# Sums of squares for the norms: four column chunks through selectors into one PSUM bank

## The chip, the cores and the metric

The kernel runs on one core of a Trainium2 chip, as one program with one launch. The metric is the device time of that execution in microseconds. Before the change three runs gave 1867.34, 1867.83 and 1867.99 us; the median is 1867.83 us.

The engines of the core are named as in the profile: PE (TensorE, matrix multiplies, with PEld for its weight loads), DVE (VectorE), ACT (ScalarE), POOL (GpSimd) and SP (SyncE, which here issues all DMA transfers, in order).

## The reference

Two layers over a residual stream of 1040 tokens (16 learned meta tokens and 1024 inputs) of width 1024.

- Layer 0: an RMS norm, one input projection, two kinds of attention side by side, a SiLU gate, an output projection and the residual add. The first attention is latent attention with 8 heads: queries and keys are made from low-rank latents which have norms of their own. The second is windowed attention over 128 tokens to each side, with 8 query heads and 2 key heads. Queries and keys of both have a norm per head.
- Layer 1: an RMS norm, an input projection, a short convolution, two gated linear recurrences (forward and backward), a SiLU gate, an output projection and the residual add.

All these norms need, for every token, the sum of the squares of a vector:

```
def rms_norm(x, g):
    xf = x.astype(jnp.float32)
    y = xf * lax.rsqrt(jnp.mean(xf * xf, axis=-1, keepdims=True) + EPS)
    return (y * g.astype(jnp.float32)).astype(x.dtype)
```

The inputs and the output are float32, and the sums must be precise.

## The kernel before, in words

**Layout.** Activations lie transposed: features on the 128 partitions, the 1040 tokens along the free dimension. A sum over features is thus a sum over partitions, and TensorE does it with a weight matrix of ones.

**Two-part numbers.** Matmuls run in a rounded float32 format. To keep precision, each operand is split into a high part and the rest (`hi`, `lo`), and a product is three matmuls; a sum of squares, whose weights are exact, needs two, one over `hi` and one over `lo`.

**Column pieces.** A PSUM bank holds 512 float32 per partition, so 1040 columns are cut in three: `C3` has 348, 346 and 346 columns, and `CH` has 272, 512 and 256 (`OFF` aligns these to banks in a three-bank tile).

**The stages**, in time: projections and up-projections of the latent attention (until about 200 us); projections, gates and the windowed attention in one mixed stream (until about 600 us); the dense latent attention with the output projection (until about 1218 us); the second layer.

**The sums of squares.** `stat(sq, s, m, dst, tag)` starts on L178. It splits the squares at once: POOL writes `sqh` (L182), VectorE writes `sql` (L183). It returns `later`, which the caller puts off: `put_off(n, fn)` and `tick()` count output tiles of the projections, so that the matmuls of the sum come one to four tiles behind. `later` then does, for each of three column pieces (L194 to L198): take a bank, two matmuls over `hi` and `lo`, one ScalarE copy of the piece into the row tile `sr`. At the end SP stores `sr` to a DRAM row (L199). `m` is 1, with a column of ones as weights (`one`), or 2, with `sel`, whose two columns select the partitions 0 to 63 and 64 to 127; there the squares of two heads have been folded into the halves by `fold`. Rows are read back in other shapes, for instance as 16 partitions of 65 tokens by `row_rsqrt` (L321) or with tokens on partitions by `tok_load` (L148) and `meta_col` (L297), get a reciprocal square root by Newton steps on VectorE (`newton_rsqrt`, L133 to L142), and go on as per-token scales.

There are 18 sums with a `tag`. Twelve belong to the first stage: input norm, two latents, shared rotary key, four query pairs and four key pairs. They use the two banks tagged `one`. Six belong to the windowed attention, namely two key norms (`d_sk`) and four query norms (`d_sq`). They use the tag `s`, whose two banks also hold the score tiles `sps` (L691 to L693). One more sum, for the second layer's norm (`d_vh`), has no tag: it uses a three-bank tile, six matmuls (`hi` first, then `lo`) and a single copy (L188 to L192).

**The order of the work.** In the first 1223 us the order on each engine is found by the framework's planner, from program order as priority and from costs of its own. Weight loads (`w_raw`, L94 to L97) and their splitting on POOL or VectorE (L115, L116) have a priority raised by 200 places. Within an engine instructions then run in that order. From the second tile of layer 1 on (L1367) the order of PE, DVE, ACT and POOL is written out by hand.

**A unit of the windowed attention** is two heads and 128 queries: scores on TensorE into `s` banks (L693), mask and maximum on VectorE (L694, L697), exponentials on ScalarE (L700, L703), reciprocal sums on VectorE (L706, L707), scaling on POOL (L710) and VectorE (L713), transposes on TensorE (L728, L731), their copies on ScalarE and VectorE (L736 to L742), and the product with the values (L753, L754). Between units TensorE does projections (`pj`, L168), whose outputs ScalarE (`qraw`, L327) or VectorE (`gt`, L783) takes out of the banks. `rope` is on L402 to L409.

Of the kernel before, what the change touches and what calls it, by code (L numbers as in the profile page):

```python
# [7 lines left out]
F32 = mybir.dt.float32  # L8
F32R = mybir.dt.float32r
# [7 lines left out]
P = 128  # L17
T = 1040
# [3 lines left out]
OFF = 240  # L22
C3 = ((0, 348), (348, 694), (694, 1040))
CH = ((0, 272), (272, 784), (784, 1040))
# [17 lines left out]
def trunk_kernel(ctx: ExitStack, tc: tile.TileContext, a: dict, out: bass.AP):  # L42
    nc = tc.nc
    wpool = ctx.enter_context(tc.tile_pool(name="wpool", bufs=3))
    xapool = ctx.enter_context(tc.tile_pool(name="xapool", bufs=16))
    const = ctx.enter_context(tc.tile_pool(name="const", bufs=1))
# [15 lines left out]
    def phase(psum_tags, **tags):  # L62

        es = ExitStack()
        stack.append(0)
        sb["P"] = es.enter_context(tc.tile_pool(name=f"ph{len(stack)}", bufs=1))
        sb["cnt"] = dict(tags)
        if psum_tags:
            psum(psum_tags)
        return es  # L70

    def row(nm, tag, dt=F32, w=T):
        if tag == "X":
            return xapool.tile([P, T], dt, tag="X", name=nm)
        return sb["P"].tile([P, w], dt, tag=tag, name=nm, bufs=sb["cnt"][tag])
# [8 lines left out]
    gqk = const.tile([P, 1], F32, name="gqk")  # L84
    nc.vector.tensor_mul(gqk, vcol(V_QKN_Q), vcol(V_QKN_K))

    ones1 = const.tile([P, 2], F32R, name="ones1")
    nc.vector.memset(ones1.bitcast(F32), 1.0)
    sel = const.tile([P, 2], F32R, name="sel")
    nc.vector.memset(sel.bitcast(F32), 0.0)  # L90
    nc.vector.memset(sel[0:64, 0:1].bitcast(F32), 1.0)
    nc.vector.memset(sel[64:128, 1:2].bitcast(F32), 1.0)

    def w_raw(src, n):  # L94
        raw = wpool.tile([P, 512], F32, tag="wr", name="wr", bufs=3)
# [59 lines left out]
    def big(nm="big"):  # L155
        return sb["ps"].tile([P, 1536], F32, tag="big", name=nm, bufs=sb["pcnt"]["big"])
# [18 lines left out]
    def bank(nm, tag):  # L175
        return sb["ps"].tile([P, 512], F32, tag=tag, name=nm, bufs=sb["pcnt"][tag])

    def stat(sq, s, m, dst, tag=None, rt="S"):  # L178

        hi = row("sqh", rt, F32R)  # L180
        lo = row("sql", rt, F32R)
        nc.gpsimd.tensor_scalar(hi, sq, 1.0, 1.0, ALU.mult, ALU.mult)  # L182
        nc.vector.tensor_sub(lo, sq, hi.bitcast(F32))  # L183

        def later():
            sr = row("sr", "T")
            if tag is None:
                ps = big("st")  # L188
                for j, x in enumerate((hi, lo)):
                    for c0, c1 in CH:  # L190
                        nc.tensor.matmul(ps[:m, OFF + c0:OFF + c1], s, x[:, c0:c1], start=j == 0, stop=j == 1)
                nc.scalar.copy(sr[:m], ps[:m, OFF:OFF + T])  # L192
            else:
                for c0, c1 in C3:  # L194
                    ps = bank("st", tag)
                    for j, x in enumerate((hi, lo)):
                        nc.tensor.matmul(ps[:m, :c1 - c0], s, x[:, c0:c1], start=j == 0, stop=j == 1)
                    nc.scalar.copy(sr[:m, c0:c1], ps[:m, :c1 - c0])  # L198
            nc.sync.dma_start(dst, sr[:m])  # L199

        return later

# [46 lines left out]

    rstd = const.tile([P, T], F32, name="rstd")  # L250
    ph = phase({"b": 2, "one": 2}, c=10, T=8, S=6, tab=2)
    one = ones1[:, 0:1]
    xh, xl, xraw = [], [], []
    w0 = {}
    sb["ahead"] = 0
# [9 lines left out]
    for k in range(8):  # L265
        h = row("xh", "X", F32R)
        lo = row("xl", "X", F32R)
# [5 lines left out]
    def proj1(e):  # L273
        ps = parts("pj")
        for hf in range(2):
            wh, wl = split_w(a["w1"][e, hf], (4, P), "w1")
            mm3p(ps, [(wh[:, k], wl[:, k], xh[4 * hf + k], xl[4 * hf + k]) for k in range(4)], hf == 0, hf == 1)
            if hf == 1:
                tick()
            yield 5.3 if hf == 0 else ps  # L280

    def run(g):
        r = None
        for v in g:
            if not isinstance(v, float):
                r = v
        return r
# [47 lines left out]
    for e in range(2):  # L335
        ps = first[3 + e]
# [49 lines left out]
    for e in range(3):  # L386
        ps = run(proj1(e))
        h = row("cqh", "c", F32R)
        lo = row("cql", "c", F32R)
# [21 lines left out]
    ps = run(proj1(5))  # L411
# [63 lines left out]
    for hf in range(2):  # L475
        wu = [split_w(a["uv"][hf, k], (512,), "wv") for k in range(2)]
        for i in range(9):
            c0, m = (0, NM) if i == 8 else (NM + P * i, P)
            ps = sb["ps"].tile([P, 512], F32, tag=f"b{i % 3}", name="vps", bufs=2)
# [426 lines left out]
    def parts_c(nm, third="t"):  # L906

        px = psC.tile([P, 1024], F32, tag="px", name="px" + nm, bufs=2)
        return [(px[:, 0:512], *C3[0]), (px[:, 512:1024], *C3[1]), (bank(nm, third), *C3[2])]
# [50 lines left out]
    for d in range(8):  # L960
        ps = parts_c("op")
# [162 lines left out]
    for d in range(1, 8):  # L1124
        ps = parts_c("op")
# [6 lines left out]
    def two(nm):  # L1132
        return sb["ps"].tile([P, 1024], F32, tag="two", name=nm, bufs=1)
# [33 lines left out]
    def halves(t, o=0):  # L1167
        return [(t[:, 0:512], o, o + 512), (t[:, 512:1024], o + 512, o + 1024)]
# [185 lines left out]
    def pair_of(nm):  # L1354
        ts = [bank(nm, "c") for _ in range(2)]
        return [(ts[j], 512 * j, 512 * j + 512) for j in range(2)]
# [170 lines left out]
    for d in range(3, 8):  # L1527
        if d % 3 == 1:
            ps = halves(two("oo"))
        elif d % 3 == 0:  # L1530
            ps = pair_of("oo")
        else:
            ps = halves(big("oo"))
# [101 lines left out]
```

## Time and profile before

| | |
|---|---|
| median of three runs | 1867.83 us |
| the profiled execution, whole | 1866.78 us |
| its span, first to last instruction | 1864.9 us |
| granted TensorE clock, mean | 0.997 |
| busy: PE / DVE / ACT / POOL | 97% / 66% / 47% / 43% |
| DMA, mean over the span | 100 GB/s |

Line numbers (L197) are those of the kernel file. A row of a waits view gives who waited, for whom, the total in us, how many times and the longest. A row of a timeline gives the start in us from the span's start, the time in us, engine, line, operation, output<-inputs, shapes, and in brackets how long the engine was idle before it and what ended that. Matmuls are pipelined: the time that one takes of TensorE is the distance between starts. A wait of PEld is a wait of the weight load, which is often hidden under the matmul before it. "PEld" and "PE" waits for the same thing are not to be added.

### The profile page before, as it was taken

How to read it: one execution, taken by the hardware profiler on the slowest of the kernel's cores; microseconds unless marked ns; L12 is line 12 of the kernel's file. 1: busy time of each engine (PE TensorE's matmuls, PEld its weight loads, DVE VectorE, ACT ScalarE, POOL GpSimd, SP SyncE). 2: the span in 40 equal slices, each digit the busy share in tenths (PEclk: the TensorE clock that was granted, in tenths of full speed). 3: DMA queues.
4: the chain of work that ended last, by engine and by line, in shares of the span. 5: the costliest groups of instructions: out<-in, count | busy, mean ns of one | idle time of the engine just before them, and what ended most of it. 6: DMA issues, size and time to landing. Idle time of an engine off the chain costs nothing.

```text
span 1864.9 us, 28561 instructions
## 1 busy us (share of the span) xinstructions
PE 1803.3 (97%) x10822; PEld 1641.8 (88%) x10822; DVE 1229.8 (66%) x1956; ACT 877.3 (47%) x1490; POOL 802.1 (43%) x713
## 2 busy tenths in 40 slices
PE   8999989989999999999999999999999999999999
PEld 7997888889999999888888889998888889988887
DVE  8687357787764641678777774348988989989000
ACT  5455224445443210466667652127776676674000
POOL 5446365354322463357555433332433433326331
PEclk9999999999999999999999999999999999999999
DMA  5355532223222363323222103422222222136421
GB/s 181 81 191 185 164 92 69 62 60 103 61 84 93 137 184 115 117 69 93 70 75 75 41 24 117 145 70 60 76 80 74 95 72 77 60 131 254 143 77 41
DMA packets 109333, 186.47 MB, mean 100 GB/s; under 512 B 31951, under 2 KB 51535, under 8 KB 109198
## 3 DMA queue, kind: packets, MB, share of 16 engines
q1 hardware_dynamic: 109198, 184.67, 31.2%
q8 instruction: 85, 1.39, 0.3%
q14 instruction: 50, 0.41, 0.1%
HBM read 126.72 MB, written 49.92 MB: 95 GB/s over the span
## 4 chain that ended last, share of the span: by engine, by line
PE 69%; DVE 16%; ACT 7%; POOL 5%; issue 2%; DMA 1%; SPq 0%; DVEq 0%; POOLq 0%; ACTq 0%
PE pj L168 12%; PE oo L168 10%; PE pxop L168 6%; PE pg L1183 5%; PE px L935 5%; PE pu L1183 5%; PE av L1026 4%; PE tp L998 3%; PE op L168 3%; PE up L168 3%; PE pz L128 2%; PE vps L435 2%; PE py L935 2%; DVE oxl L769 1%; DVE oz L1287 1%
## 5 line engine op out<-in xcount | busy, mean ns | idle before, releaser
L116 POOL TENSOR_TENSOR wl<-wr,wh 128x512 fp32r<-128x512 f32 (+2 forms) x218 | 320.8, 1475 | 301.9 <-ACT wh L113 269.8
L115 POOL TENSOR_SCALAR wh<-wr 128x512 fp32r<-128x512 f32 (+2 forms) x157 | 121.6, 775 | 376.0 <-PE pj L168 124.4
L168 PE MATMUL pj<-xh,wl 128*128 128x346 f32 (+1 forms) x768 | 251.3, 328 | 14.3 <-DVE wl L116 7.8
L168 PE MATMUL pj<-xl,wh 128*128 128x346 f32 (+1 forms) x768 | 249.1, 324 | 0.9 <-DVE xl L269 0.8
L168 PE MATMUL pj<-xh,wh 128*128 128x346 f32 (+1 forms) x768 | 248.9, 324 | 0.0
L168 PEld LDWEIGHTS pj<-xh,wl 128*128 128x128 f32 x768 | 146.5, 191 | 16.1 <-ACT xh L268 7.7
L168 PEld LDWEIGHTS pj<-xl,wh 128*128 128x128 f32 x768 | 146.6, 191 | 2.0 <-DVE xl L269 1.9
L168 PEld LDWEIGHTS pj<-xh,wh 128*128 128x128 f32 x768 | 146.6, 191 | 0.1
L1183 PE MATMUL pu<-h1h,wl 128*128 128x346 f32 (+1 forms) x384 | 125.2, 326 | 6.3 <-DVE ou L1201 3.3
L1183 PE MATMUL pu<-h1l,wh 128*128 128x346 f32 (+1 forms) x384 | 123.5, 322 | 0.0
L1183 PE MATMUL pu<-h1h,wh 128*128 128x346 f32 (+1 forms) x384 | 123.4, 321 | 0.0
L1013 ACT CAST pth<-tp 128x512 fp32r<-128x512 f32 (+1 forms) x160 | 77.9, 507 | 66.2 <-PE tp L998 52.3
L1014 DVE TENSOR_TENSOR ptl<-tp,pth 128x512 fp32r<-128x512 f32 (+1 forms) x160 | 90.2, 585 | 19.9 <-ACT pth L1013 16.4
L1183 PE MATMUL pg<-h1h,wl 128*128 128x512 f32 x256 | 101.4, 396 | 0.0
L168 PE MATMUL oo<-oyh,wh 128*128 128x512 f32 x256 | 101.1, 395 | 0.0
L1183 PE MATMUL pg<-h1h,wh 128*128 128x512 f32 x256 | 101.1, 395 | 0.0
L1183 PE MATMUL pg<-h1l,wh 128*128 128x512 f32 x256 | 100.8, 394 | 0.0
L168 PE MATMUL oo<-oyh,wl 128*128 128x512 f32 x256 | 100.6, 393 | 0.0
L168 PE MATMUL oo<-oyl,wh 128*128 128x512 f32 x256 | 100.4, 392 | 0.0
L944 ACT ACTIVATE p<-py,mmx,msc 128x256 f32<-128x256 f32 (+1 forms) x72 | 40.8, 567 | 119.0 <-DVE mmx L942 102.3
L1351 DVE TENSOR_TENSOR hres<-oo,hres 128x512 f32<-128x512 f32 x16 | 10.6, 688 | 129.0 <-PE oo L168 129.0
L998 PE MATMUL tp<-ident,p 128*128 128x128 f32 (+1 forms) x576 | 90.5, 275 | 2.7 <-POOL p L955 1.9
(446 smaller groups left out, 5471.2 us busy)
## 6 DMA issues: line engine op xcount, KB each, us to landing
wr<-in_w SPq DMA_DIRECT2D x128, 256.0 KB
wr<-in_wo SPq DMA_DIRECT2D x64, 256.0 KB
s_g<-gth SPq DMA_DIRECT2D x10, 520.0 KB
xr<-in_x SPq DMA_DIRECT2D x8, 520.0 KB
s_qn<-qr SPq DMA_DIRECT2D x8, 520.0 KB
s_kn<-kr SPq DMA_DIRECT2D x8, 520.0 KB
sw<-qraw SPq DMA_DIRECT2D x16, 260.0 KB
yb<-s_yb SPq DMA_DIRECT2D x8, 520.0 KB
```

The costliest lines, as they stand in the source:

```text
L115: eng.tensor_scalar(hi[:, :n], raw[:, :n], 1.0, 1.0, ALU.mult, ALU.mult)
L116: eng.tensor_sub(lo[:, :n], raw[:, :n], hi[:, :n].bitcast(F32))
L128: nc.tensor.matmul(ps[:m, off + c0:off + c1], w, x[:, c0:c1], start=first and j == 0 and pi == 0, stop=last and j == nt - 1 and pi == 2)
L168: nc.tensor.matmul(t[:, :c1 - c0], w, x[:, c0:c1], start=first and j == 0 and pi == 0, stop=last and j == nt - 1 and pi == 2)
L435: nc.tensor.matmul(ps[:m, :n], s, w, start=j == 0 and pi == 0, stop=j == nt - 1 and pi == 2)
L935: nc.tensor.matmul(dst[:m, d0:d0 + a1 - a0], l[:, s], r[:, a0:a1], start=pi == 0, stop=pi == 4)
L944: nc.scalar.activation(p_[:m, b0:b1], ps, AF.Exp, bias=mx[:m, 2:3], scale=sc, accum_out=mx[:m, 3 + z:4 + z])
L998: nc.tensor.transpose(tp[:, o:o + m], p_[:m, NM + P * (kt + j):NM + P * (kt + j) + P], ident[:m, :m])
L1013: nc.scalar.copy(hi[:, :w], tp[:, :w])
L1014: nc.vector.tensor_sub(lo[:, :w], tp[:, :w], hi[:, :w].bitcast(F32))
L1026: nc.tensor.matmul(av[:, :n], l[:, vs], pts[kt][o][:, j * n:j * n + n], start=kt == 0 and j == 0 and pi == 0, stop=False)
L1183: nc.tensor.matmul(t[:, :c1 - c0], l, r[:, c0:c1], start=hf == 0 and k == 0 and pi == 0, stop=hf == 1 and k == 3 and pi == 2)
```

## The change

`later` cuts the 1040 columns into four chunks of 260. All four go into one bank, on different partitions: the weights for chunk j are a selector matrix of 4 columns (m = 1) or 8 columns (m = 2) in which only column j, or the columns j and 4 + j, are not zero. A matmul with such a selector writes the sums of chunk j to partition j (and 4 + j) and adds zero to the other partitions, so that eight matmuls accumulate in one group and leave the 1040 sums as 4 or 8 rows of 260. One ScalarE copy takes them out, and one store writes 4 or 8 rows of 1040 bytes to the same DRAM rows as before. The sum of the second layer's norm, which had one copy of 1040 columns, takes the same way, in the first bank of its three-bank tile; its order of `hi` and `lo` now alternates by chunk. The row tile `sr` is asked for behind the matmuls. The selectors are set up at the start by 14 memsets instead of 4.

```
-    ones1 = const.tile([P, 2], F32R, name="ones1")
-    nc.vector.memset(ones1.bitcast(F32), 1.0)
-    sel = const.tile([P, 2], F32R, name="sel")
+
+    one = const.tile([P, 4, 4], F32R, name="one")
+    nc.vector.memset(one.bitcast(F32), 0.0)
+    sel = const.tile([P, 4, 8], F32R, name="sel")
     nc.vector.memset(sel.bitcast(F32), 0.0)
-    nc.vector.memset(sel[0:64, 0:1].bitcast(F32), 1.0)
-    nc.vector.memset(sel[64:128, 1:2].bitcast(F32), 1.0)
+    for j in range(4):
+        nc.vector.memset(one[:, j, j:j + 1].bitcast(F32), 1.0)
+        nc.vector.memset(sel[0:64, j, j:j + 1].bitcast(F32), 1.0)
+        nc.vector.memset(sel[64:128, j, 4 + j:5 + j].bitcast(F32), 1.0)
...
         def later():
-            sr = row("sr", "T")
             if tag is None:
                 ps = big("st")
-                for j, x in enumerate((hi, lo)):
-                    for c0, c1 in CH:
-                        nc.tensor.matmul(ps[:m, OFF + c0:OFF + c1], s, x[:, c0:c1], start=j == 0, stop=j == 1)
-                nc.scalar.copy(sr[:m], ps[:m, OFF:OFF + T])
             else:
-                for c0, c1 in C3:
-                    ps = bank("st", tag)
-                    for j, x in enumerate((hi, lo)):
-                        nc.tensor.matmul(ps[:m, :c1 - c0], s, x[:, c0:c1], start=j == 0, stop=j == 1)
-                    nc.scalar.copy(sr[:m, c0:c1], ps[:m, :c1 - c0])
-            nc.sync.dma_start(dst, sr[:m])
+                ps = bank("st", tag)
+            for j in range(4):
+                for z, x in enumerate((hi, lo)):
+                    nc.tensor.matmul(ps[:4 * m, :260], s[:, j], x[:, 260 * j:260 * j + 260],
+                                     start=j == 0 and z == 0, stop=j == 3 and z == 1)
+            sr = row("sr", "T")
+            nc.scalar.copy(sr[:4 * m, :260], ps[:4 * m, :260])
+            nc.sync.dma_start(dst.rearrange("m (j c) -> (m j) c", c=260), sr[:4 * m, :260])
...
-    one = ones1[:, 0:1]
```

## The prediction

> **What bounds the kernel now.** I read the page first, then the waits of TensorE, then every instruction on the tile `st` (the bank of the sums), then the timeline around single sums.
>
> ```profile
> span 1864.9 us, 28561 instructions
> PE 1803.3 (97%) x10822; PEld 1641.8 (88%) x10822; DVE 1229.8 (66%) x1956; ACT 877.3 (47%) x1490; POOL 802.1 (43%) x713
> PE 69%; DVE 16%; ACT 7%; POOL 5%; issue 2%; DMA 1%; SPq 0%; DVEq 0%; POOLq 0%; ACTq 0%
> PE st L197 <- ACT sr L198: 5.6, 5, 2.1
> PE pj L168 <- ACT qraw L327: 4.5, 2, 4.3
> PE st L197 <- DVE sql L183: 3.8, 3, 1.7
> ```
>
> TensorE is busy for 97% of the span and carries 69% of the chain that ended last. The last three rows are its own longest waits that matter here (us in total, times, longest). The first and the third stand at the sums: 5.6 us until ScalarE has copied a bank out, and 3.8 us until VectorE has made the low half `sql`. Only the first is touched. So the waits that the change can remove from TensorE add up to 5.6 us, 0.30% of the span, and the question is how much of that reaches the end.
>
> The operations at issue (the view of the tile `st`; ns are min/median/max):
>
> ```profile
> L198 ACT COPY sr<-st x54: 422/436/443, 46.2 to 478.9; 2x346 f32<-2x346 f32 x24, 1x346 f32<-1x346 f32 x12, 2x348 f32<-2x348 f32 x12, 1x348 f32<-1x348 f32 x6
> L192 ACT COPY sr<-st x1: 1017/1017/1017, 1225.7 to 1225.7; 1x1040 f32<-1x1040 f32 x1
> ```
>
> 54 copies are 18 sums of three; with the copy at L192 there are 19 sums. By the calls in the code twelve of the 18 belong to the stage before 200 us and six (two key norms, four query norms) to the window attention.
>
> **ScalarE's copies.** These two kinds of copy give the slope: (1017 - 436) / (1040 - 346) = 0.84 ns a column, so 260 columns are an estimated 436 - 86 x 0.84 = 364 ns. ScalarE saves 54 x 0.436 - 18 x 0.364 = 17.0 us and 0.65 us at L192. It is busy for 47%, so this counts only where something waits for it.
>
> **TensorE's own work.** A sum streams 2080 columns before and after, in eight pieces instead of six. The cost of a piece is the distance between starts, not its duration:
>
> ```profile
> 91.15 0.32 PE L168 MATMUL up<-cql,wh 128*128 128x348 f32 x1
> 91.37 0.32 PE L197 MATMUL st<-sqh,ones 128*1 128x346 f32 x1
> 91.52 0.32 PE L197 MATMUL st<-sql,ones 128*1 128x346 f32 x1
> 417.06 0.28 PE L753 MATMUL av<-ph,svh 128*128 128x256 f32 x1
> 417.18 0.28 PE L753 MATMUL av<-pl,svh 128*128 128x256 f32 x1
> 1231.61 0.39 PE L1183 MATMUL pg<-h1l,wh 128*128 128x512 f32 x1
> 1231.84 0.40 PE L1183 MATMUL pg<-h1h,wh 128*128 128x512 f32 x1
> ```
>
> 256 columns take 0.12 us and 512 take 0.23, so 260 take about 0.12. For 346 the line through these two gives 0.159 and the rows 0.15 (91.37 to 91.52); I take 0.157: 8 x 0.12 = 0.96 us against 6 x 0.157 = 0.94, +0.02 us a sum, +0.24 us for the twelve sums before 200 us, where TensorE is the limit. Eight selector columns instead of two are no cost: the 256-column rows run at 0.12 us with 128 columns of weights.
>
> [...]
>
> The same rows show a small gain: the third bank starts 0.22 us after the matmul before it, 0.06 late, because its weight load waits for the first copy. Bounds over twelve sums are 0 and 12 x 0.06 = 0.72 us; with half of them showing it, -0.36 us. Together this stage gives about -0.1 us.
>
> **The window attention, where the large waits are.** One of them, whole:
>
> ```profile
> 414.00 0.28 PE L753 MATMUL av<-ph,svl 128*128 128x256 f32 x1
> 416.40 0.32 PE L197 MATMUL st<-sqh,ones 128*1 128x346 f32 x1 [2.12 <-ACT sr L198]
> 416.75 1.22 DVE L713 TENSOR_SCALAR sp<-sp,ssm 128x416 f32<-128x416 f32 x2
> 418.00 1.37 DVE L783 SCALAR_TENSOR_TENSOR gt<-pj,rstd 128x348 f32<-128x348 f32 x3
> 418.83 0.60 PE L728 MATMUL tA<-ident,sp 128*128 128x128 f32 x4
> 419.29 0.72 DVE L694 CUSTOM_DVE_ANT_0 sp<-sps,masks,vec 128x432 f32<-128x432 f32 x1
> PE tA L728 <- DVE nw_t L140: 1.1, 1, 1.1
> DVE ssm L706 <- ACT sp L703: 2.8, 6, 0.9
> DVE sp L713 <- POOL spm L710: 0.5, 1, 0.5
> DVE gth L786 <- ACT gth L785: 0.3, 1, 0.3
> ```
>
> The third bank can start only when the copy of the first is done, and that copy stands behind a unit's exponentials in ScalarE's queue. After the change the eight matmuls run at once and TensorE goes on. But to what? The transposes `tA` (418.83) need VectorE's L713, which ends at 417.97 either way; then VectorE does L783 up to 419.37 without a pause. The last four rows are waits between 390 and 430 us: TensorE waits again for VectorE soon after, and VectorE in this stretch (392 to 428) waits for ScalarE's exponentials and for POOL, never for TensorE. The copies are queued behind those exponentials, so they do not hold VectorE either. TensorE would arrive earlier and wait longer at the next transposes. Bounds for removing the 5.6 us: 0 and -5.6 us; nearest to the rows is 0, and I take 0. The cover is VectorE's chain; were it gone, the whole 5.6 us would count.
>
> **The store.** Its source becomes four rows of 1040 B (eight with two heads) instead of one or two of 4160 B; the loads behind it do not change. One store sets a long wait, that of the first key norm:
>
> ```profile
> 247.82 0.43 ACT L198 COPY sr<-st 1x346 f32<-1x346 f32 x1
> 249.47 0.33 SPq L96 DMA_DIRECT2D wr<-in_w  x1
> 249.89 0.24 SPq L199 DMA_DIRECT2D d_sk<-sr  x1
> 252.18 0.33 SPq L321 DMA_DIRECT2D t<-d_sk  x1
> 254.39 0.34 DVE L322 SCALAR_TENSOR_TENSOR t<-t,e 16x65 f32<-16x65 f32 x1 [6.80 <-DMA t<-d_sk]
> 258.59 0.31 SPq L324 DMA_DIRECT2D d_rks<-nw_y  x1
> 259.96 0.34 SPq L152 DMA_DIRECT2D rkb<-d_rks  x1
> ```
>
> The load of `t` is next in SP's queue and waits for the store: 252.18 - 249.89 = 2.29 us with one row of 4160 B. The same step with sixteen rows of 260 B (L324 to L152) takes 1.37 us. Four rows of 1040 B lie between, so the gain is 0 to 0.92 us; the new row is four times one and a quarter of the other, so I take the middle, -0.45 us. VectorE idles 6.80 us for this load, its rsqrt chain holds up the rope of `qraw`, and TensorE's wait of 4.3 us for ScalarE's `qraw` copy hangs on it, so the gain arrives. That the sum is done earlier gives nothing here: its last copy ends at 248.25, but the store is issued straight behind the weight load `wr`, which goes out at 249.47 when a buffer is free.
>
> **At no cost or gain.** The sum at 1225 us: its copy shrinks by 0.65 us, and only one of the eight matmuls can run ahead of `sql` instead of three of six, but the store is held by SP:
>
> ```profile
> 1225.44 1.29 POOL L116 TENSOR_TENSOR wown<-wr,wown 128x512 fp32r<-128x512 f32 x1
> 1225.66 1.02 ACT L192 COPY sr<-st 1x1040 f32<-1x1040 f32 x1 [4.82 <-PE st L191]
> 1226.75 0.33 SPq L96 DMA_DIRECT2D wr<-in_w  x1
> 1227.13 0.28 SPq L199 DMA_DIRECT2D d_vh<-sr  x1
> 1.27 0.06 DVE L647 MEMSET ssc<- 128x1 f32 x1
> 2.76 0.16 DVE L85 TENSOR_TENSOR gqk<-vec 128x1 f32<-128x1 f32 x1 [1.40 <-DMA vec<-in_vec]
> ```
>
> The load at 1226.75 goes out when POOL ends (1226.73), 0.07 us after the copy. An earlier copy still finds SP there; without that cover it would be worth up to 0.65 us of a chain that TensorE does not wait for. The ten added memsets (fourteen for four) fall into VectorE's 1.40 us of idle time ahead of 2.76 us (last row); at 0.06 us each (the row above it) they are 0.6 us, at twice that 1.2, and both fit. The 3.8 us wait for `sql` stays: its matmul is still second in the sum.
>
> **The sum.** -0.1 (first stage) + 0 (window attention, PE waits) - 0.45 (store) + 0 = -0.6 us, on a profiled execution of 1866.78 us (span 1864.9 plus 1.9 around it), which lies 1.05 us under the median of 1867.83. On the median: 1867.2 us. Alone this case holds 1865.5 to 1869.
>
> **Rivals.**
> *The waits reach the end* (faster). If VectorE is not the limit between its waits, the whole 5.6 us counts, with the 0.6 above: 1867.8 - 6.2 = 1861.6. For it: the 97% of the page; against it: VectorE's waits above name no TensorE.
> *The store overtakes the weight load in SP's queue* (faster). The planner now sees a sum finished about two copies (0.87 us) earlier and may issue the store ahead of `wr`. Here that is worth 249.89 - 248.25 = 1.64 us on the chain behind `t`, and as much again if a second sum does it: 1867.2 - 3.3 = 1863.9. Against it: `wr` has a priority raised by 200.
> *VectorE's order gets worse* (slower). Up to 1223 us the planner orders all engines from its own costs, and these change. A query norm's rsqrt chain then becomes ready earlier in its model and is put ahead of a unit's softmax:
>
> ```profile
> 288.16 0.18 DVE L136 TENSOR_SCALAR nw_y<-ssc 128x17 int32<-128x17 int32 x1
> 290.50 0.17 DVE L653 TENSOR_SCALAR ssc<-nw_y 128x17 f32<-128x17 f32 x1
> ```
>
> One such chain is 2.5 us (288.16 to 290.67) of the engine that limits this stage. One lies within what counts as no change, two decide: 1867.2 + 5.0 = 1872.2. Against it: a sum stays ten instructions (6 + 3 + 1 before, 8 + 1 + 1 after), so the planner's order of priorities is nearly kept.
> *The change moves the wait instead of removing it* (the next score tile wants the bank that the sum still holds): TensorE's 5.6 us reappear at `sps`. That ends within 0.5 us of the forecast and is counted with it.
>
> **Chances.** Forecast 0.45, waits reach the end 0.24, store overtakes 0.12 (half of it beyond 0.2%), VectorE's order 0.19. A measurement of this kernel tells about 0.2% (3.7 us) from no change. Faster 0.24 + 0.06 + a little from odd orders = 0.32, same 0.48, slower 0.20. The range must reach both ends: 1861.2 to 1872.0.
>
> **What would show it.** Right: copies of the sums 18 and near 0.36 us; eight `st` matmuls 0.12 us apart; the row "PE st <- ACT sr" gone; TensorE's waits for `sp` and `smx` grown by most of 5.6 us; `t<-d_sk` issued 1.4 to 2.3 us behind its store. Wrong: the page's TensorE idle time falls by over 4 us, the order of instructions on VectorE differs between 280 and 500 us, or matmul starts at 260 columns lie clearly over 0.12 us apart.

## The result, and the profile after

The changed kernel takes 1879.81 us (median of four runs, 1878.52 to 1882.55); the kernel before took 1867.59 us beside it. The ratio is 1.0068, 95% interval 1.0054 to 1.0082: slower by 12.2 us, where no change was forecast.

The page of the changed kernel (span and busy times), and its rows for the tile `st`:

```profile
span 1876.7 us, 28608 instructions
PE 1809.3 (96%) x10860; PEld 1648.4 (88%) x10860; DVE 1214.7 (65%) x1966; ACT 862.2 (46%) x1454; POOL 804.5 (43%) x713
...
L195 PE MATMUL st<-sqh,sel x48: 277/282/288, 109.3 to 487.4; 128*8 128x260 f32 x48
...
L198 ACT COPY sr<-st x19: 351/365/368, 46.4 to 1237.5; 8x260 f32<-8x260 f32 x12, 4x260 f32<-4x260 f32 x7
```

What the change does directly is as forecast: 19 copies of 0.365 us instead of 55, and ScalarE is busy for 862.2 us instead of 877.3. The span is 11.8 us longer all the same. The waits of TensorE in the changed kernel:

```profile
PE tA L727 <- DVE sp L712: 9.6, 17, 1.6
...
PE sps L692 <- DVE qm L635: 3.5, 1, 3.5
...
PE tA L727 <- DVE nw_y L144: 2.9, 1, 2.9
PE up L171 <- DVE kr L326: 2.9, 2, 2.6
...
PE st L195 <- DVE sql L186: 2.6, 4, 1.2
...
PE sps L692 <- ACT sr L198: 1.9, 3, 1.5
...
PE st L195 <- POOL sqh L185: 1.7, 1, 1.7
```

The row "PE st <- ACT sr" (5.6 us before) is gone. In its place stand several waits for VectorE that were smaller or absent before (`qm`, `nw_y`, `kr`), and more at `tA` (6.4 us before). The score tiles `sps` now wait 1.9 us for the one copy.

Where the time is lost is read from the last start of the same matmuls, stage by stage. The rows, of before and then of after (ns are min/median/max, then the first and last start in us):

```profile
L168 PE MATMUL up<-cqh,wh x108: 314/320/326, 82.1 to 169.5; 128*128 128x346 f32 x72, 128*128 128x348 f32 x36
L753 PE MATMUL av<-pl,svh x92: 177/280/388, 302.2 to 593.2; 128*128 128x256 f32 x88, 128*128 128x32 f32 x4
```

```profile
L171 PE MATMUL up<-cqh,wh x108: 317/321/493, 81.9 to 173.2; 128*128 128x346 f32 x72, 128*128 128x348 f32 x36
L752 PE MATMUL av<-pl,svh x92: 177/281/388, 307.6 to 603.7; 128*128 128x256 f32 x88, 128*128 128x32 f32 x4
```

`up` starts 0.2 us earlier than before and ends 3.7 us later, so the first loss lies between 82 and 170 us. `vps`, the projection of the values just before the window attention, has its last start at 227.2 us instead of 223.1, 4.1 us later, and the window attention (`av`) ends 10.5 us later, so the second and larger loss lies in the window attention. Matched one by one, equal matmuls jump by +2.9 us near 125 us and by another 6 us between 420 and 500 us; some 3 us more come in smaller steps between and behind.

**What changed there.** Outside the sums and the set-up of their selectors the two kernels issue the same instructions, but the planner has put them in another order. The places at which the two sequences differ (of the ordered part, sums left out):

```
            TensorE  VectorE  ScalarE  GpSimd  SyncE's transfers
places           61      171       38      12                 80
```

An instruction that has moved mostly counts twice here, where it stood and where it stands now, and the expectations of e12 to e15 count in the same way. By the order of starts in the two traces, one sequence becomes the other when about 32 instructions of TensorE, 94 of VectorE, 21 of ScalarE, 6 of GpSimd and 43 transfers move.

The first jump in the changed kernel (VectorE's timeline; in brackets the idle time ahead of an instruction and what ended it), and TensorE at the same sum:

```profile
114.86 2.06 DVE L406 TENSOR_TENSOR sw<-sw,tabS 128x1040 f32<-128x1040 f32 x1
...
118.20 1.77 DVE L457 TENSOR_TENSOR qs<-qs,qs 128x1040 f32<-128x1040 f32 x1
...
122.10 0.29 PE L195 MATMUL st<-sqh,sel 128*8 128x260 f32 x1 [1.70 <-POOL sqh L185]
123.55 0.28 PE L195 MATMUL st<-sql,sel 128*8 128x260 f32 x1 [1.17 <-DVE sql L186]
```

The same place in the kernel before (that add is L458 there, the rope's first operation L407 at 117.45 us):

```profile
115.88 1.23 DVE L458 TENSOR_TENSOR qs<-qs,qs 128x1040 f32<-128x1040 f32 x1
...
122.82 0.48 PE L197 MATMUL st<-sql,sel 128*2 128x348 f32 x2 [1.70 <-DVE sql L183]
```

The rope of a head (L406, L407) now stands ahead of the add that finishes the squares (L457), which runs at 118.20 us; before, that add ran at 115.88 us, ahead of the rope. TensorE stands at the sum twice, for `sqh` and for `sql`; before it stood there once, for 1.70 us. And behind the wait its clock is halved (columns: stretch, its length, busy us and instructions of PE, PEld, DVE, ACT, POOL, then the granted clock; after, then before):

```profile
121.10:124.51 3.41, 1.24 (x9) 0.86 (x10) 2.46 (x5) 0.00 (x0) 2.91 (x3) 1.00 0.68 233
124.51:127.93 3.42, 3.42 (x14) 3.42 (x13) 0.69 (x2) 3.28 (x6) 0.00 (x0) 0.50 0.53 183
```

```profile
121.36:124.77 3.41, 1.95 (x13) 1.74 (x14) 3.18 (x3) 1.31 (x4) 3.33 (x4) 1.00 0.00 0
124.77:128.19 3.42, 3.42 (x23) 3.42 (x22) 1.24 (x1) 3.29 (x6) 1.15 (x3) 1.00 0.96 347
```

The stretches after 124.5 us hold 14 matmuls in the one and 23 in the other. The first jump is thus 1.70 + 1.17 - 1.70 = 1.17 us more of waiting and up to 3.41 / 2 = 1.7 us of half clock, 2.9 us together. Up to 1700 us the kernel before has three such stretches of 3.41 us at half clock and the changed one five. The two more are worth up to 2 x 3.41 / 2 = 3.4 us of the 11.8. TensorE's idle time by the two pages grows by 5.8 us (1876.7 - 1809.3 = 67.4 us against 1864.9 - 1803.3 = 61.6); the other 2.6 us lie in its busy time, whose ends are modelled, and are not told apart.

### The profile page after: what moved, and what is told of

Its sections match the earlier page's. It is cut to its first block, busy times and chain, and to the rows that moved or that the text cites. A ratio compares the mean times of both kernels' runs of the same rounds, so it can differ in the third digit from the quotient of the medians.

```text
span 1876.7 us, 28608 instructions
## 1 busy us (share of the span) xinstructions
PE 1809.3 (96%) x10860; PEld 1648.4 (88%) x10860; DVE 1214.7 (65%) x1966; ACT 862.2 (46%) x1454; POOL 804.5 (43%) x713
## 4 chain that ended last, share of the span: by engine, by line
PE 56%; DVE 12%; ACT 7%; POOL 4%; DMA 2%; issue 1%; SPq 1%; DVEq 0%; ACTq 0%; POOLq 0%
PE pj L171 9%; PE oo L171 8%; PE pxop L171 6%; PE px L934 6%; PE pg L1182 5%; PE pu L1182 4%; PE av L1025 4%; PE tp L997 3%; PE op L171 3%; PE py L934 2%; PE pz L131 2%; DVE oz L1286 1%; DVE oxl L768 1%; DVE oz L1293 1%; DVE oz L1291 1%
## 5 line engine op out<-in xcount | busy, mean ns | idle before, releaser
L119 POOL TENSOR_TENSOR wl<-wr,wh 128x512 fp32r<-128x512 f32 (+2 forms) x218 | 325.5, 1497 | 301.5 <-ACT wh L116 265.3
L118 POOL TENSOR_SCALAR wh<-wr 128x512 fp32r<-128x512 f32 (+2 forms) x157 | 116.5, 743 | 382.7 <-PE pj L171 123.9
```

The lines of the kernel that those rows point to most:

```text
L118: eng.tensor_scalar(hi[:, :n], raw[:, :n], 1.0, 1.0, ALU.mult, ALU.mult)
L119: eng.tensor_sub(lo[:, :n], raw[:, :n], hi[:, :n].bitcast(F32))
```

## The experiments

Two theories at first. **A**: the loss is the planner's new sequence of everything else. **B**: the new sums cost it themselves (selectors of eight columns, one bank for four chunks, a store of rows cut in four).

To hold a sequence, each instruction of an engine is made to follow the one ahead of it in a written list, in issue order only (no semaphore is added), up to layer 1's second tile. The change to a kernel is this, and the experiments e1, e2, e5 to e11 and e16 to e18 differ in the lists:

```
+def pin_order(tc):
...
+        for j, k in zip(order, order[1:]):
+            tc.add_manual_dep(mine[k], mine[j].name,
+                              mybir.DependencyInfo(mybir.DependencyClass.NoSync, mybir.DependencyReason.DATA),
+                              reason="pin_order")
...
+            pin_order(tc)
             ET = mybir.EngineType
```

### e1: the new sums in the old sequence

The changed kernel with the lists of the kernel before.

> The new sums as in the changed kernel, but every other instruction of the five engines held in the sequence it had before the change, up to layer 1's second tile; each new sum's matmuls stand where the old sum's first matmul of the second operand stood, its one copy where the first of the three copies stood, its store where the old one stood. Theory A (the loss is the planner's new sequence of everything else: VectorE's adds and rsqrt steps, the rope's swap loads on SyncE): 1866.5 to 1868.5 us, ratio 0.999 to 1.001, and the offset of equal TensorE matmuls against the kernel before stays within 1 us to the end. Theory B (the new sums themselves cost it: selectors of eight columns, one bank for four chunks, a store of rows cut in four): 1878 to 1881 us, ratio 1.006 to 1.007, with the jumps at 125 and 436 us still there.

Measured: 1867.24 us, ratio 0.9998 (0.9989 to 1.0008). Theory A holds and B falls: the whole loss goes with the sequence. One part of A's expectation fails: equal matmuls do not stay within 1 us of the kernel before. They come 0.7 us early at 40 us, 2.8 us early near 480 us, and level from 1500 us on. TensorE's waits in e1:

```profile
PE tA L727 <- DVE sp L712: 10.1, 16, 1.8
...
PE st L195 <- DVE sql L186: 4.8, 4, 1.8
```

Without the distraction of a new sequence the change does what the forecast said of it: the 5.6 us at `st` for ScalarE are gone, `tA` for `sp` has grown from 6.4 to 10.1 us, and the time stays. The interval is 2 us wide to either side, so effects of a few tenths are not told from nothing. The changed kernel with its own lists, as a control of the lists themselves, was not run; e1 shows that holding a list costs nothing there.

### e2: the old sums in the new sequence

The kernel before with the lists of the changed kernel.

> The sums of the kernel before (twelve or six matmuls, three copies or one, the old selectors and store), with everything else held in the sequence that the changed kernel has up to layer 1's second tile. Theory A (sequence): 1877 to 1881 us, ratio 1.005 to 1.007. Theory B (the new sums themselves): 1867 to 1869 us, ratio 0.999 to 1.001.

Measured: 1895.68 us, ratio 1.0154 (1.0139 to 1.0169). Slower, as A says, but 14 us beyond its range, so A in its plain form is too simple: a sequence fits the sums that it was made for. The old sum needs three copies where the new sequence has room for one, and TensorE waits for them (5.6 us in the kernel before):

```profile
PE st L197 <- ACT sr L198: 19.4, 17, 2.9
```

### e3 and e4: the new sums in one stage only, planned anew

```
         def later():
+            if not (tag == "one"):      # e4: "s"
...                                       the sum as it was before
```

> New sums in the first stage's ten norms alone (those whose banks are of the kind of the projections there); the eight sums of the window attention's units and the last one as before the change. The planner orders the rest anew. Theory A: the jump near 125 us comes back and stays, those at 436 and 490 us need not: +3 to +5 us, 1871 to 1873 us, ratio 1.0016 to 1.0027. Theory B: ten of nineteen sums, so about half of the 12 us, +6 us, 1873 to 1875 us.

> New sums for the eight sums of the window attention's units alone, the first stage's and the last as before the change. The planner orders the rest anew. Theory A: no loss before 280 us, the jumps between 420 and 500 us come back: +5 to +8 us, 1873 to 1876 us, ratio 1.003 to 1.0045. Theory B: eight of nineteen sums, +5 us, spread evenly over the eight places, about 0.6 us at each; by theory A the loss stands at two or three places instead.

Measured: e3 1874.27 us, 1.0037 (1.0024 to 1.0050); e4 1875.32 us, 1.0045 (1.0028 to 1.0061). The traces show twelve sums in the new form in e3 and six in e4, not the ten and eight of the expectations. The last starts, read from the same kind of rows as above:

| last start of | before | after | e1 | e3 | e4 |
|---|---|---|---|---|---|
| `up` (first stage) | 169.5 | 173.2 | 169.0 | 173.2 | 169.4 |
| `vps` | 223.1 | 227.2 | 223.0 | 227.2 | 223.0 |
| `av` (window attention) | 593.2 | 603.7 | 592.0 | 597.6 | 601.3 |
| `pu` (second layer) | 1661.2 | 1672.3 | 1661.2 | 1667.3 | 1668.5 |

Each stage's new sums bring that stage's loss: 3.7 us for the first in e3 and 8.1 us for the window attention in e4. For the window attention that is more than the changed kernel loses there itself (10.5 - 4.1 = 6.4 us): the two halves of the change don't add up. In all, e3 lies above A's range of 1871 to 1873 us (another 1.7 us arise between `av` and `pu`) and within B's, which e1 has ruled out; e4 lies in A's range.

### e5 and e16: the jump near 125 us

e5 is e1 with one block of seven instructions of VectorE in the changed kernel's sequence. The two rope operations go ahead of the add, as the expectation says; the block also puts the rope's third operation ahead of `sql` and two copies out of the projections' banks (`kr`) behind it. e16 moves two weight splits of GpSimd (two instructions each) too. The lists, as source lines:

```
 VectorE                              GpSimd (e16 only)
 -kr                  L326            +wh, wl              L118, L119
 +sw = sw * tabS      L406            +wh, wl              L118, L119
 +qr = qr * tabC      L407             sqh                 L185
  qs = qs + qs        L457            -wh, wl, wh, wl
 -kr, sw, qr
 +qr = qr + sw        L408
  sql                 L186
 -qr = qr + sw
 +kr, kr              L326
```

> The kernel of e1_new_sums_old_order (new sums, old sequence, 1867.24 us) with one inversion of the changed kernel's on VectorE put back: at 115 us the first two rope operations (sw x tabS, qr x tabC) stand ahead of the add that finishes the squares of a query pair, instead of behind it. Theory C (this one inversion makes the loss near 125 us): the squares come 3.2 us later, TensorE waits 1.5 to 2.5 us more at the sum near 120 us, and if the clock is halved for 3.41 us behind that wait 1.7 us more; kept to the end, 1868.7 to 1871.5 us. Rival (it takes the many other moved instructions too, or the loss is caught up by 200 us): within 1 us of 1867.24.

> The kernel of e5_rope_ahead (1869.62 us), with GpSimd's sequence of the changed kernel near 113 to 120 us as well: two weight splits (wh, wl) stand ahead of the sum's sqh there. In the changed kernel a rope operation took 2.06 us beside such a split, in e5 1.24 us with GpSimd idle. Theory G (the loss near 125 us needs both, VectorE's inversion and GpSimd's splits beside it): TensorE's matmuls behind 125 us come 1.5 to 3 us later than in e1, rope operations of 1.8 to 2.1 us appear near 115 us, 1869.5 to 1872 us in all. Rival (the splits ahead only use idle time of GpSimd): within 1 us of e5 at 125 us and in all.

Measured: e5 1869.62 us, 1.0011 (1.0001 to 1.0020); e16 1870.92 us, 1.0019 (1.0009 to 1.0028). e5's time is in the range of theory C, but not for C's reason: equal matmuls lose only 0.6 us against e1 at 120 us. In e16 they lose 3.6 us there, 0.6 more than theory G allowed, and the loss stays until 300 us, with the clock halved near 125 us as in the changed kernel (mean granted clock 0.53 from 125.03 to 128.44 us). e5, then e16:

```profile
114.02 1.24 DVE L406 TENSOR_TENSOR sw<-sw,tabS 128x1040 f32<-128x1040 f32 x1
...
116.32 1.24 DVE L457 TENSOR_TENSOR qs<-qs,qs 128x1040 f32<-128x1040 f32 x1
117.65 1.98 POOL L185 TENSOR_SCALAR sqh<-qs 128x1040 fp32r<-128x1040 f32 x1 [7.41 <-DVE qs L457]
121.68 0.43 PE L171 MATMUL up<-cqh,wl 128*128 128x348 f32 x1 [1.72 <-DVE kr L326]
```

```profile
113.71 1.02 POOL L119 TENSOR_TENSOR wl<-wr,wh 128x384 fp32r<-128x384 f32 x1
113.75 2.07 DVE L456 TENSOR_TENSOR qs<-qs,qs 128x1040 f32<-128x1040 f32 x1 [0.17 <-ACT qs L438]
...
118.25 1.77 DVE L457 TENSOR_TENSOR qs<-qs,qs 128x1040 f32<-128x1040 f32 x1
122.14 0.28 PE L195 MATMUL st<-sqh,sel 128*8 128x260 f32 x1 [1.97 <-POOL sqh L185]
124.03 0.43 PE L171 MATMUL up<-cqh,wl 128*128 128x348 f32 x1 [1.60 <-DVE kr L326]
```

With GpSimd idle for 7.41 us, VectorE's rope operations and adds on 1040 columns take 1.23 to 1.24 us each. Beside GpSimd's splits one takes 2.07 and one 1.77 us, and the squares are finished at 120.02 us instead of 117.56; 0.9 us of that the execution of e16 was late from its start, so 1.6 us are the splits'. In e1 TensorE waits once here, 1.82 us for `sql`. In e5 it waits 0.39 us for `sqh` and 1.72 us for a bank that `kr` empties, hardly more; in e16 1.97 and 1.60 us, 1.75 us more than in e1, and the half clock adds up to 1.7 us. So the first jump is made by the two moves together, as theory G says. The splits alone were not run, and neither was the rope without the two copies. In the changed kernel itself the second wait near 124 us is for `sql`; there TensorE waits for `kr` at 145.8 us, for 2.56 us.

### e6, e7, e9, e17, e18: the jump between 420 and 500 us

All are e1 with parts of the changed kernel's sequence put in: e7 the whole stage on four engines; e6 two blocks of VectorE alone; e18 only the first of them; e9 three instructions of it; e17 the block without these three. The first block, as source lines (`L739`, `L705`, `L693` are the three of e9):

```
-pl - tB   L739, ssm  L705, mask+max  L693
 gate product gth   L785
 t (row of squares) L321
+ssm  L705, mask+max  L693, pl - tB  L739, with Newton steps between
 scalings of sp     L712
...
-three Newton steps  L142 to L144
-ssm, ssm  L705, reciprocal  L706
 pl - tA            L736
+Newton step, pl - tB  L739, Newton step, ssm  L705, Newton step, ssm  L705, reciprocal  L706
+spmr - tB          L741
 scalings of sp     L712
-pl - tB  L739, and further down spmr - tB  L741
```

> The kernel of e1_new_sums_old_order with the changed kernel's sequence on TensorE, VectorE, ScalarE and GpSimd from 280 us to the end of the window attention; the first stage and SyncE stay in the old sequence. Theory A (sequence, by stages): the part of the loss that arises behind 280 us comes back, +6 to +8 us, 1873 to 1875.5 us, without the jump near 125 us. Rival (SyncE's sequence or the first stage's delay is needed for it): under +3 us.

> The kernel of e1_new_sums_old_order with VectorE's sequence of the changed kernel in two short blocks alone: near 428 to 440 us and near 495 to 502 us the Newton steps of a query norm stand ahead of, or between, the reciprocals, scalings and subtractions of a unit's softmax. Theory C (rsqrt steps ahead of the softmax make the later loss): TensorE's waits for sp and tA grow there, +2 to +5 us, 1869 to 1872 us. Rival (the steps are 0.2 us each and the unit has slack): within 1 us of 1867.24.

> The kernel of e1_new_sums_old_order (1867.24 us) with three VectorE instructions moved: near 420 us one subtraction (pl<-tB), one partial sum (ssm) and one mask-and-maximum (sp<-sps) of the softmax stand behind the gate's product gth and the row t instead of ahead of them, as in the changed kernel. In e6 VectorE stood idle there for 1.59 us until ScalarE had made gth, with these three ready behind. Theory D (head-of-line: VectorE's order puts an instruction that waits for ScalarE ahead of ready softmax steps): +3 to +5 us, 1870 to 1872.5 us, with an idle row of 1 to 2 us ahead of gth. Rival (in e6 it was the Newton steps between the softmax steps): under +1.5 us.

> The kernel of e1_new_sums_old_order with VectorE's sequence of the changed kernel in the block near 428 to 440 us, but with the three softmax steps of e9 left ahead of the gate's product, and the block near 495 us left old. So the Newton steps between the softmax steps alone. e6 (both blocks) was 11.4 us above e1, e9 (the three steps behind the gate) 2.8. Theory H (the effects add up): the rest, +5 to +8 us, 1872 to 1875 us. Rival (it is the combination that costs): under +3 us, 1867 to 1870 us.

> As e17, with the three softmax steps behind the gate's product as well, so e6 without its block near 495 us. Theory H (effects add up, the block near 495 us does little): e17 plus 2.8 us, near 1877 us. Rival (combination): 1874 us or more although e9 and e17 each stay under 1870.5. Third way (the block near 495 us carried it): under 1871 us.

| | moved | us | above e1 | ratio to before, 95% |
|---|---|---|---|---|
| e7 | stage, four engines | 1878.14 | 10.9 | 1.0046 to 1.0076 |
| e6 | VectorE, both blocks | 1878.64 | 11.4 | 1.0050 to 1.0082 |
| e18 | VectorE, first block | 1875.84 | 8.6 | 1.0029 to 1.0059 |
| e17 | first block less three | 1874.90 | 7.7 | 1.0024 to 1.0054 |
| e9 | the three alone | 1870.04 | 2.8 | 1.0001 to 1.0020 |

The window attention's part is VectorE's sequence: the blocks of VectorE alone cost as much as the whole stage. The sizes of e6 and e7 were underestimated. e9 comes out between the rival's bound of 1.5 us and the 3 us of theory D; the idle row that D named is there. e17 and e18 say that most lies in the rest of the first block, roughly adding up (7.7 with 2.8 is 10.5, measured 8.6, with intervals of some 3 us on each side). Matched with e1, TensorE's matmuls show it in place: between 420 and 440 us they lose 1.1 us in e9, 4.8 us in e17 and 6.0 us in e18. The rest of each total arises elsewhere, part of it ahead of the block, where the lists are those of e1 (1.6 us near 315 us in e17, whose profile has a mean clock of 0.994, that of e1 0.999), and is not the block's. e9, then e17, then e1 (VectorE, with ScalarE's second sum of exponentials):

```profile
420.35 0.68 DVE L736 TENSOR_TENSOR pl<-tA,ph 128x512 fp32r<-128x512 f32 x1
422.59 1.25 DVE L785 SCALAR_TENSOR_TENSOR gth<-gth,gt 128x1040 f32<-128x1040 f32 x1 [1.56 <-ACT gth L784]
423.89 0.41 DVE L739 TENSOR_TENSOR pl<-tB,ph 128x256 fp32r<-128x256 f32 x1
```

```profile
430.67 0.19 ACT L702 ACTIVATION_READ_ACCUMULATOR sp<-sp,snm 128x1 f32 x1
431.36 0.69 DVE L736 TENSOR_TENSOR pl<-tA,ph 128x512 fp32r<-128x512 f32 x1 [2.29 <-ACT ph L735]
432.57 0.20 DVE L705 TENSOR_SCALAR ssm<-ssm,ses 128x1 f32<-128x1 f32 x1
433.06 0.17 DVE L706 RECIPROCAL ssm<-ssm 128x2 f32<-128x2 f32 x1
433.89 0.42 DVE L741 TENSOR_TENSOR spmr<-tB,spmr 32x256 fp32r<-32x256 f32 x1 [0.67 <-ACT spmr L740]
434.34 1.91 DVE L712 TENSOR_SCALAR sp<-sp,ssm 128x416 f32<-128x416 f32 x2
435.04 0.30 PE L727 MATMUL tA<-ident,sp 128*128 128x128 f32 x1 [2.06 <-DVE sp L712]
436.39 0.52 PE L727 MATMUL tA<-ident,sp 128*128 128x128 f32 x3 [1.05 <-DVE sp L712]
```

```profile
427.51 0.19 ACT L702 ACTIVATION_READ_ACCUMULATOR sp<-sp,snm 128x1 f32 x1
427.73 0.21 DVE L705 TENSOR_SCALAR ssm<-ssm,ses 128x1 f32<-128x1 f32 x1 [0.28 <-ACT sp L702]
427.98 0.17 DVE L706 RECIPROCAL ssm<-ssm 128x2 f32<-128x2 f32 x1
428.20 0.69 DVE L736 TENSOR_TENSOR pl<-tA,ph 128x512 fp32r<-128x512 f32 x1
428.81 1.14 DVE L712 TENSOR_SCALAR sp<-sp,ssm 128x416 f32<-128x416 f32 x2
```

In both kernels ScalarE finishes the exponentials and then casts `ph`. In e1 VectorE sums and inverts at once, and the scaling for which TensorE waits starts 1.1 us behind the exponentials (427.70 to 428.81). In e17 the subtraction that needs `ph` stands first: VectorE is idle for 2.29 us, the last 0.50 of them with the sums ready behind it (430.86 to 431.36). Then come the second subtraction (L739) and Newton steps of 0.20 us between the sums, VectorE is idle for another 0.67 us at the subtraction for `spmr` (L741), and the scaling starts 3.5 us behind (430.86 to 434.34). So an instruction out of place costs its own time (0.2 us for a Newton step, 0.4 for L741) and the time that VectorE stands still at it.

### e10: mending the changed kernel

The changed kernel's own lists, with VectorE's blocks near 115, 428 to 440 and 495 to 502 us from the kernel before.

> The changed kernel in its own sequence on all five engines, but on VectorE four short blocks of 7, 20, 14 and 26 instructions (near 115 us, 428 to 440 us and 495 to 502 us) in the sequence of the kernel before. Theory C and D (these places carry most of the loss): 1869 to 1873 us instead of 1879.81. Rival (the loss is spread over the 200 and more moved instructions): 1876 to 1880 us.

Measured: 1883.45 us, 1.0080 (1.0064 to 1.0097): slower than the changed kernel, so both expectations fall. The mean clock of its profile, 0.990, is the lowest of all: up to 1700 us eleven stretches of 3.41 us ran at half clock, in the changed kernel five, and the six more are worth up to 10.2 us. TensorE's idle time is what it was, 67.8 us against 67.4. So no waiting was saved, and what e10 lost it lost by the clock; why the clock was halved more often was not followed. The other engines are still sequenced for the blocks that were taken out, which may be the reason but is not shown to be. That blocks put into the old sequence cost what the change costs (e16 +3.7 and e18 +8.6 us above e1, together 12.3; the changed kernel +12.6) doesn't make them removable one by one. No run has both blocks and nothing else, and with e6 or e7 in the place of e18 the sum would be 15.1 or 14.6 us.

### e8 and e11: can the new sums be made to pay?

Both are e1 with a place mended by hand where its trace shows TensorE waiting. e8 moves three sums of the first stage back on TensorE by 14, 5 and 8 matmuls; e11 puts softmax steps first at five places.

> The kernel of e1_new_sums_old_order with three sums of the first stage moved back on TensorE: the eight matmuls of the sums near 122, 144 and 152 us stand 14, 5 and 8 matmuls later, where by the trace of e1 the low half of the squares is ready. There TensorE waited 1.82, 1.44 and 1.1 us for it. Theory (TensorE is the limit in this stage, so the work put under the wait counts): -1.5 to -3.5 us, 1863.7 to 1865.7 us, faster than both kernels. Rival (the projections that TensorE reaches earlier wait for banks that VectorE and ScalarE free): within 1 us of 1867.24.

> The kernel of e1_new_sums_old_order with five places of the window attention where VectorE or GpSimd does something else while the softmax step for which TensorE waits is ready: near 422 us the gate's product and six Newton steps go behind the scalings of sp, near 464 us the halves of the squares (sqh, sql) go behind the scalings, near 480 us the gate's product goes behind the subtractions, near 345 us nine Newton steps go behind a mask-and-maximum, near 312 us sql and qm go behind the copy spmr. By the trace of e1 TensorE waited there 1.7, 1.95, 1.9, 1.8 and 2.35 us, 9.7 in all. Theory (VectorE's sequence sets TensorE's time in this stage, so the same lever works the other way): half of it or more arrives, -3 to -7 us, 1860 to 1864.5 us, under both kernels. Rival (each gain is taken by the next wait, as in e8): within 1.5 us of 1867.24.

Measured: e8 1868.15 us, 1.0004 (0.9994 to 1.0013); e11 1869.69 us, 1.0013 (1.0004 to 1.0023). Neither gains. In e8 the rival holds: the waits for `sql` fall from 4.8 to 2.1 us, and the wait for the banks that VectorE empties takes their place (0.7 us in e1):

```profile
PE up L171 <- DVE kr L326: 2.3, 3, 0.9
...
PE st L195 <- DVE sql L186: 2.1, 4, 0.8
```

In e11 the theory fails by 5 us or more, and the rival's bound of 1.5 us is passed too. Matched with e1, its matmuls are 0.3 us ahead at 300 us and 1.0 us behind at 590 us, so the mended places gain nothing in sum; another 2.9 us are lost between 700 and 900 us, behind all five places. The mean clock of its profile is 0.997, in e1 0.999. Why is not settled. No version faster than the kernel before was found.

### e12 to e15: is it the new sums, or any new sequence?

The sums' matmuls, copies and stores get a priority 10 places higher or 20 lower; nothing else is edited. e12 and e13 have the old sums, e14 and e15 the new ones.

```
         def later():
+            with tc.high_priority(10):      # e13, e15: -20
```

> The kernel before, its sums untouched, but their matmuls, copies and stores have a priority raised by 10 places, so that the planner orders anew: outside the sums 57 instructions of TensorE, 120 of VectorE and 38 transfers of SyncE move (the change under study moved 61, 171 and 80). Theory E (the sequence of the kernel before is a good draw, and any new one of the planner's costs about as much): 1871 to 1882 us. Rival F (it is the new sums in the planner's model that lead it astray; old sums nudged stay): 1866 to 1870 us.

> As e12, with the priority of the old sums lowered by 20 places: 49 instructions of TensorE, 141 of VectorE and 60 transfers move. Theory E: 1871 to 1882 us. Rival F: 1866 to 1870 us.

> The changed kernel with the priority of its new sums raised by 10 places: against the changed kernel 29 instructions of TensorE and 105 of VectorE move. Theory E (a draw among orders): anywhere from 1869 to 1885 us, and the two nudged kernels with new sums lie on average within 4 us of the two with old sums. Rival F (the new sums mislead the planner): 1876 to 1884 us, above both kernels with old sums nudged.

> The changed kernel with the priority of its new sums lowered by 20 places: against the changed kernel 17 instructions of TensorE and 139 of VectorE move. Theory E: anywhere from 1869 to 1885 us. Rival F: 1876 to 1884 us, above both kernels with old sums nudged.

| | sums | us | ratio to before, 95% |
|---|---|---|---|
| e12 | old, +10 | 1873.28 | 1.0016 to 1.0040 |
| e13 | old, -20 | 1878.58 | 1.0043 to 1.0073 |
| e14 | new, +10 | 1876.85 | 1.0033 to 1.0063 |
| e15 | new, -20 | 1875.50 | 1.0030 to 1.0059 |

Theory E holds and F falls. Old sums with another sequence cost 5.9 and 11.2 us, new ones 9.5 and 8.1; the means, 1875.9 and 1876.2 us, lie closer together than the two runs of either kind. The kernel before has a sequence that is better than every other of the planner's that was tried here, and the changed kernel lost that, not anything that the sums do. Why each of these sequences is slower was not followed in their traces.

## Why the prediction was wrong

**Right: the parts.** The copies take 0.365 us (estimate 0.364), matmul starts at 260 columns lie 0.12 us apart (123.67, 123.79, 123.91 us in the changed kernel), "PE st <- ACT sr" is gone, and TensorE meets it again at the transposes. With the old sequence held, the whole is 1867.24 us against a forecast of 1867.2. That it is so close is luck: the terms of the sum are at most half a microsecond, e1's interval is 2 us to either side, and one term was not found (next paragraph). The rival "the waits reach the end" is out: e1 has no gain. "The store overtakes" is not tested by e1, which holds the old place of the store; in the changed kernel the store of `d_sk` at 254.04 us still goes out behind the weight loads (`wr`, from 247.02 us).

**The store** was sized at -0.45 us. From the store of `d_sk` to the load of `t` it is 1.89 us in the changed kernel, but 2.31 us in e1 with the same store (2.29 before). A gain from four shorter rows is not shown.

**The step that failed** is the sentence that set the chance of the fourth rival: "a sum stays ten instructions (6 + 3 + 1 before, 8 + 1 + 1 after), so the planner's order of priorities is nearly kept". The same number of instructions did not keep it: some 94 instructions of VectorE moved (171 places). A nudge by ten places, with no instruction changed, moved some 65 (120 places). The forecast rested on that step, since every row it used was read from a sequence that the changed kernel no longer has.

**The rival "VectorE's order gets worse"** named the mechanism and the stage: Newton steps of a norm among a unit's softmax, between 280 and 500 us. Its price was too low in three terms. It counted only a chain's own time, 2.5 us; in e18 one block with one chain cost 8.6 us, 6.0 of them at the block, since VectorE also stands still for ScalarE at the misplaced instruction. It left out the first stage (3.7 us in e16). And it did not know of the halved clock (up to 3.4 us of the 11.8). The range, up to 1872.0, ended where two chains at that price did, and the forecast gave this side 0.20.

## What to carry to other kernels

Where a planner orders the engines, as here, a local edit can be a new draw of the whole order. Its price is read from other draws: nudge a priority in the kernel as it is, and take the spread (here +5.9 to +11.2 us) as the uncertainty of any edit, before the edit's own microseconds are summed. To learn what an edit itself is worth, hold the old sequence around it; an order that has turned out well is best kept in writing.

## What the runs showed of the hardware

**Where the clock was halved.** In the kernel before:

```profile
312.50:315.92 3.42, 1.27 (x12) 1.06 (x11) 3.35 (x6) 2.67 (x4) 2.35 (x3) 1.00 0.36 96
315.92:319.33 3.41, 3.41 (x13) 3.41 (x13) 2.78 (x5) 1.34 (x5) 3.06 (x2) 0.50 0.70 175
466.10:469.52 3.42, 1.23 (x7) 0.73 (x6) 2.55 (x5) 0.00 (x0) 1.88 (x4) 1.00 0.05 7
469.52:472.93 3.41, 3.41 (x15) 3.39 (x14) 2.51 (x5) 0.96 (x2) 3.41 (x2) 0.50 0.31 82
```

Each halved stretch lasted 3.41 us. In the 3.42 us ahead of each TensorE was busy for 1.27 or 1.23 us, and for 0.69 us ahead of the third (264.72 us); with 1.95 us (121.36 us, above) the clock stayed whole. In the changed kernel the times of TensorE ahead of its five are 1.24 us (121.10 us), 0.42 (264.46), 0.15 (281.53), 0.86 (428.30) and 1.50 (476.09). These rows set no bound. Two waits of nearly the same length in the kernel before ended differently: behind one of 2.15 us (`tB`, until 315.12 us) the clock was halved, worth up to 1.7 us more, and behind one of 2.12 us (`st`, until 416.40 us) it stayed whole.

**VectorE beside GpSimd.** An operation on 128x1040 took 1.24 us with GpSimd idle (e5 above) and up to 2.07 us beside its splits (e16 above). In the whole kernel before, the 33 tensor-tensor operations of VectorE on 1040 float32 columns that ran beside no operation of GpSimd took 1.22 to 1.24 us, and the 59 that ran beside one took 1.22 to 3.4 us. From e5 to e16 only GpSimd's splits were moved, and the same add (L457) went from 1.24 to 1.77 us.
